# First projections of a two-block network: loaded, ordered and multiplied tile by tile of x

## The chip, the core and the metric

The kernel runs on one core of a Trainium2 chip. The core has five engines that work beside each other, each through its own queue in order: PE (matrix products; PEld is its weight load), DVE (vector work), ACT (activation functions, copies with a scale), POOL (a second, slower vector engine) and SP, which issues most loads here. Sixteen DMA engines move the data. The metric is device time in microseconds from the first to the last instruction of one execution and what lies around it, as the median of several runs.

## What is computed

Two blocks in a row on x of 512 tokens and 1024 channels, all in fp32. The first block has two layers of the following kind; the second block (a recurrence beside sparse attention) does not touch the change.

```python
n = rmsnorm(h, attn_norm[l])
proj = n @ w_in[l]
u, v_sgu, q, k, v_att = split(proj)          # 512 columns each
y_sgu = sgu_mixer(gelu(u), gelu(v_sgu), ...)
y_att = diff_attention(rope(q), rope(k), v_att, ...)   # 4 heads, two maps of 64 each
h = h + concat(y_sgu, y_att) @ w_out[l]
h = h + conv_ffn(rmsnorm(h, ffn_norm[l]), ...)
```

In `rmsnorm` each token's row is divided by its root mean square. The kernel multiplies first and applies that factor, which is one number per token, to the products afterwards.

## The kernel before, in words

x is held transposed as `h`, eight tiles of 128 channels by 512 tokens. Products are made in a fast fp32 format: every operand is split into a high part and a low part, and `mm3` makes three products (high by high, high by low, low by high) that add up in one PSUM bank. So each weight passes through `prep` (line 257 and after): SP loads 128 x 1024 into `raw`, POOL writes the high part `whi` (`gscale`, line 204), DVE subtracts to get the low part `wlo` (`tt`, line 192). There are three buffers of each of the three. A tile of x is split in `split_scaled`: ACT writes the high part with the norm's gain (line 298), DVE the low part (line 197). `Next` (line 771) does that for a tile and adds the tile's squares to a running sum (ACT squares, POOL adds, DVE adds the last).

The kernel is written for a planner: instructions get a priority by their place in the program, `tc.high_priority(offset=...)` moves a stretch ahead by that many places (nested offsets add up; `prep` has 260), and the planner puts, on each engine, the ready instruction with the best priority next. On the chip each engine then keeps that order. Tiles with the same tag take turns in so many buffers.

`program` first loads the columns `vec` and the first tile of x at a high priority, and the rest of `vec`. `enter(stack, "one", ...)` gives the first block eight PSUM banks: three `mm`, two `sc`, two `tr`, one `o`. Then, at line 779, a loop loads the other seven tiles of x and calls `Next` on all eight. `mixer` for layer 0 begins with the tables of the rotation (`tables`, DVE and ACT); `fm` multiplies queries and keys of head 0 over all eight tiles of x into the two `sc` banks (line 569); `norm_row` sums the squares over channels with four small products (`columns`, line 333), takes root and reciprocal (`rstd_col`, lines 336 and 337: the column `rc`) and spreads it to rows with four transposes (`spread`, line 358); ACT copies the result to `R` (line 573). The rotation tables CR and SR are multiplied by R (DVE, POOL). `q_of` and `k_of` rotate: `rope` copies the product, shuffles it, multiplies by CR and SR and adds, in buffers with the tag `rp`, of which there are four; the result is split again, and `stacked` (lines 431, 432) moves the halves with small loads into tiles with the tag `QK`, of which there are twelve. After that the values: 96 products, four token tiles by eight tiles of x, into three `mm` banks and the `o` bank; ACT copies them out scaled by `rc` (line 589) and DVE makes the low part.

Then the steps of `STEPS` are written: `k1` makes queries and keys of head 1 in `mm` banks, `a0` is the attention of head 0 (its scores at lines 450 and 451, in `sc` banks), `a1` that of head 1, `v0` the first half of the gate (`gate_half`, two `mm` banks), and so on. `silu_c` (lines 613 to 615) is a small vector that the second block's modulation needs later.

Of the kernel before, what the change touches and what calls it, by code (L numbers as in the profile page):

```python
# [5 lines left out]
F32 = mybir.dt.float32  # L6
# [3 lines left out]
ALU = mybir.AluOpType  # L10
# [134 lines left out]
def program(tc, a, at, out):  # L145
# [3 lines left out]
    def nm(s):  # L149
        count[0] += 1  # L150
        return f"{s}_{count[0]}"

    import contextlib
    with contextlib.ExitStack() as ctx:
# [13 lines left out]
        def bank(tag="mm"):  # L168
            return scope["ps"].tile([P, 512], F32, tag=tag, name=nm(tag), bufs=scope["banks"][tag])

        def t2(tag, dt=F32R):
            return tl([P, 512], dt, tag)
# [23 lines left out]
        def stt(o, i0, s, i1, op0, op1, **kw):  # L196
            latest[0] = V.scalar_tensor_tensor(o, i0, s, i1, op0, op1, **kw)  # L197
# [5 lines left out]
        def gscale(o, i, s, plus=0.0):  # L203
            G.tensor_scalar(o, i, s, plus, op0=ALU.mult, op1=ALU.add)  # L204

        def fr(ap):
            return ap.bitcast(F32)
# [2 lines left out]
        h = ctile([P, KD, S], "h")  # L210
        vec = ctile([P, a["vec"].shape[1]], "vec")
        with tc.high_priority(offset=5000):
            nc.sync.dma_start(vec[:, 0:KD], a["vec"][:, 0:KD])
            nc.sync.dma_start(h[:, 0, :], a["x"][:, 0, :])

        nc.sync.dma_start(vec[:, KD:], a["vec"][:, KD:])

        def col(n, j=0, w=1):
            return vec[:, at[n] + j:at[n] + j + w]
# [7 lines left out]
        with tc.high_priority(offset=5000):  # L227
            G.memset(eps, EPS)
            A.activation(eps[:, 1:2], eps[:, 0:1], AF.Sin)
        eps = eps[:, 0:1]  # L230

        AHEAD = 260
        HALVES = slice(0, 256), slice(256, 512)
# [42 lines left out]
        def mm3(o, sh, sl, mh, ml, first, last):  # L276
            T.matmul(o, sh, mh, start=first, stop=False)  # L277
            T.matmul(o, sh, ml, start=False, stop=False)  # L278
            T.matmul(o, sl, mh, start=False, stop=last)  # L279
# [13 lines left out]
        def fm(src, X, tag="mm"):  # L293
            return fm_group([src], X, [tag])[0]
# [176 lines left out]
        def recurrence_constants():  # L471
# [23 lines left out]
            V.tensor_scalar(hb[:, 0:4], col("lru_ba", 0, 4), 0.5, None, op0=ALU.mult)  # L495
            V.tensor_scalar(hb[:, 4:8], col("lru_bx", 0, 4), 0.5, None, op0=ALU.mult)


        def mixer(l, X, sums, on_h):
            li = LAM_INIT[l]  # L500
# [65 lines left out]
                    tt(V, OT[hd], OT[hd], spread(SL[:, 4 * hd:4 * hd + 4], "o"), ALU.mult)  # L566


            oq = fm(a[f"w_q{l}"][0], X, "sc")
            ok = fm(a[f"w_k{l}"][0], X, "sc")  # L570
            rc, Rp = norm_row(sums, "tr")
            R = row()
            A.copy(R, Rp)
            tt(V, CR, CR, R, ALU.mult)
            tt(G, SR, SR, R, ALU.mult)
            qks = q_of(oq), k_of(ok)
            os = [bank(t) for t in ("mm", "mm", "mm", "o")]
            for c in range(4):
                w = prep(a[f"w_va{l}"][c])
                for kk in range(2):  # L580
                    k = 2 * c + kk
                    for t in range(NT):
                        tok = slice(t * P, t * P + P)
                        n = slice(kk * 512, kk * 512 + 512)
                        mm3(os[t], X[k][0][:, tok], X[k][1][:, tok], w[0][:, n], w[1][:, n], k == 0, k == KD - 1)
            VA = []
            for t in range(NT):
                hi, lo = t2("V"), t2("V")
# [18 lines left out]
            A.activation(lv[:, 2:4], lv[:, 0:2], AF.Exp)  # L607
            tt(V, lv[:, 4:5], lv[:, 3:4], lv[:, 2:3], ALU.subtract)
            V.tensor_scalar(lv[:, 5:6], lv[:, 4:5], -li, None, op0=ALU.add)
            V.tensor_scalar(lv[:, 6:7], col(f"subln{l}"), 1.0 - li, None, op0=ALU.mult)  # L610
            nlam, sub = lv[:, 5:6], lv[:, 6:7]
            if l == 0:
                A.activation(silu_c, col("c", 0, KD), AF.Tanh, scale=0.5)
                stt(silu_c, silu_c, 1.0, col("c", 0, KD), ALU.add, ALU.mult)
                V.tensor_scalar(silu_c, silu_c, 0.5, None, op0=ALU.mult)

            VT = []

# [152 lines left out]
        class Next:  # L771
# [3 lines left out]
            def __call__(self, m):  # L775
                self.X[m] = split_scaled(h[:, m, :], col(self.gain, m), "X")
                self.sums.square(h[:, m, :])

        nx = Next("attn_norm0")
        for m in range(KD):  # L780
            if m > 0:
                nc.sync.dma_start(h[:, m, :], a["x"][:, m, :])
            nx(m)
        fin = [None, None]

        def last(m, ts=slice(0, 512)):
# [586 lines left out]
```

## Time and profile before

| | |
|---|---|
| median of 3 runs | 1817.63 us (1812.58 to 1818.64) |
| the profiled execution | 1814.92 us |
| its span, first to last instruction | 1813.3 us |
| PE busy | 1737.3 us (96%) |
| DVE, POOL, ACT busy | 1253.4, 808.4, 588.2 us |

Busy times of the engines overlap. PE is near its whole span, so what matters is where it is not busy, or busy at half its clock. A line of the timeline reads: start, duration (of the whole run of instructions where there are several), engine, line, operation, output tile <- input tiles, shapes, count, and in brackets how long the engine was idle before and what ended that.

### The profile page before, as it was taken

How to read it: one execution, taken by the hardware profiler on the slowest of the kernel's cores; microseconds unless marked ns; L12 is line 12 of the kernel's file. 1: busy time of each engine (PE TensorE's matmuls, PEld its weight loads, DVE VectorE, ACT ScalarE, POOL GpSimd, SP SyncE). 2: the span in 40 equal slices, each digit the busy share in tenths (PEclk: the TensorE clock that was granted, in tenths of full speed). 3: DMA queues.
4: the chain of work that ended last, by engine and by line, in shares of the span. 5: the costliest groups of instructions: out<-in, count | busy, mean ns of one | idle time of the engine just before them, and what ended most of it. 6: DMA issues, size and time to landing. Idle time of an engine off the chain costs nothing. (4 is left out here: it accounts for less than half of the span.)

```text
span 1813.3 us, 23607 instructions
## 1 busy us (share of the span) xinstructions
PE 1737.3 (96%) x8422; PEld 1448.9 (80%) x8422; DVE 1253.4 (69%) x1957; ACT 588.2 (32%) x1120; POOL 808.4 (45%) x791
## 2 busy tenths in 40 slices
PE   7999999999999999999999999899898899999997
PEld 5887778888887888787888887878776788888886
DVE  7677788868877578769868967655876872444344
ACT  3464332113123256332203213344774431201022
POOL 5553554346446454444426626322461752323233
PEclk9999999999999999999999999899999899999998
DMA  4552255657745453245567756375331223323331
GB/s 174 155 140 94 93 185 175 215 189 232 252 152 173 133 150 93 96 132 177 176 216 233 235 175 192 105 251 192 129 116 49 104 82 104 93 94 98 99 94 58
DMA packets 104117, 267.74 MB, mean 148 GB/s; under 512 B 12481, under 2 KB 15553, under 8 KB 104001
## 3 DMA queue, kind: packets, MB, share of 16 engines
q1 hardware_dynamic: 104000, 266.25, 46.5%
q8 instruction: 66, 1.08, 0.2%
q14 instruction: 51, 0.41, 0.1%
HBM read 213.77 MB, written 35.65 MB: 138 GB/s over the span
## 5 line engine op out<-in xcount | busy, mean ns | idle before, releaser
L204 POOL TENSOR_SCALAR whi<-raw 128x1024 fp32r<-128x1024 f32 (+3 forms) x266 | 313.9, 1185 | 630.8 <-PE mm L278 227.3
L192 DVE TENSOR_TENSOR wlo<-raw,whi 128x1024 fp32r<-128x1024 f32 (+3 forms) x264 | 383.9, 1456 | 186.7 <-POOL whi L204 171.5
L277 PE MATMUL mm<-X,whi 128*128 128x512 f32 (+1 forms) x688 | 261.9, 386 | 6.6 <-ACT X L298 2.0
L279 PE MATMUL mm<-X,wlo 128*128 128x512 f32 (+1 forms) x688 | 261.7, 383 | 5.1 <-DMA wlo<-parts 2.8
L278 PE MATMUL mm<-X,whi 128*128 128x512 f32 (+1 forms) x688 | 263.9, 385 | 1.0 <-DVE X L197 1.0
L197 DVE SCALAR_TENSOR_TENSOR p<-p,vec,p 128x512 f32<-128x512 f32 x176 | 183.8, 1066 | 4.2 <-ACT p L711 3.3
L277 PEld LDWEIGHTS mm<-X,whi 128*128 128x128 f32 x688 | 130.2, 192 | 32.7 <-ACT X L298 2.6
L279 PEld LDWEIGHTS mm<-X,wlo 128*128 128x128 f32 x688 | 131.7, 192 | 30.3 <-DVE wlo L192 4.4
L278 PEld LDWEIGHTS mm<-X,whi 128*128 128x128 f32 x688 | 131.7, 191 | 25.3 <-DVE X L197 2.6
L277 PE MATMUL sc<-X,whi 128*128 128x512 f32 (+1 forms) x376 | 143.3, 383 | 7.3 <-POOL whi L204 7.2
L711 ACT ACTIVATE p<-p,vec 128x512 f32<-128x512 f32 x88 | 69.9, 813 | 241.6 <-DVE p L192 236.4
L279 PE MATMUL sc<-X,wlo 128*128 128x512 f32 (+1 forms) x376 | 141.6, 380 | 5.4 <-DVE wlo L192 4.4
L278 PE MATMUL sc<-X,whi 128*128 128x512 f32 (+1 forms) x376 | 142.2, 379 | 0.0
L192 POOL TENSOR_TENSOR pt<-pt,pt 128x512 fp32r<-128x512 f32 x64 | 109.9, 1719 | 62.6 <-ACT pt L250 62.3
L277 PE MATMUL tr<-X,whi 128*128 128x512 f32 x280 | 108.9, 389 | 0.0
L278 PE MATMUL tr<-X,whi 128*128 128x512 f32 x280 | 108.9, 389 | 0.0
L279 PE MATMUL tr<-X,wlo 128*128 128x512 f32 x280 | 107.6, 390 | 0.0
L277 PEld LDWEIGHTS sc<-X,whi 128*128 128x128 f32 x376 | 72.2, 192 | 20.5 <-POOL whi L204 7.8
L279 PEld LDWEIGHTS sc<-X,wlo 128*128 128x128 f32 x376 | 71.5, 191 | 21.2 <-DVE wlo L192 8.5
L455 ACT ACTIVATE p<-p,sa 128x128 f32<-128x128 f32 (+3 forms) x128 | 71.6, 561 | 51.0 <-DVE sa L453 50.5
L192 POOL TENSOR_TENSOR p<-p,p 128x512 f32<-128x512 f32 x44 | 60.7, 1379 | 58.7 <-ACT p L718 37.2
L278 PEld LDWEIGHTS sc<-X,whi 128*128 128x128 f32 x376 | 71.9, 191 | 12.7
(691 smaller groups left out, 4014.6 us busy)
## 6 DMA issues: line engine op xcount, KB each, us to landing
parts<-pt SPq DMA_DIRECT2D x128, 256.0 KB, 3.9
raw<-in_w_f_dram SPq DMA_DIRECT2D x64, 512.0 KB, 3.7
vt<-in_ada_dram SPq DMA_DIRECT2D x96, 256.0 KB, 3.0
raw<-in_w_g_dram SPq DMA_DIRECT2D x44, 512.0 KB, 3.5
raw<-in_w_v_dram SPq DMA_DIRECT2D x44, 512.0 KB, 4.2
raw<-in_w_d_dram SPq DMA_DIRECT2D x32, 512.0 KB, 4.2
whi<-parts SPq DMA_DIRECT2D x32, 512.0 KB, 3.4
wlo<-parts SPq DMA_DIRECT2D x32, 512.0 KB, 4.2
```

The lines of the kernel that those rows point to most:

```text
L192: i = e.tensor_tensor(o, i0, i1, op=op)
L197: latest[0] = V.scalar_tensor_tensor(o, i0, s, i1, op0, op1, **kw)
L204: G.tensor_scalar(o, i, s, plus, op0=ALU.mult, op1=ALU.add)
L277: T.matmul(o, sh, mh, start=first, stop=False)
L278: T.matmul(o, sh, ml, start=False, stop=False)
L279: T.matmul(o, sl, mh, start=False, stop=last)
L455: A.activation(p[i], p[i], AF.Exp, bias=m, scale=-1.0, accum_out=Z[:, z0 + i:z0 + i + 1])
L711: A.activation(y, t[:, 0:512], AF.Identity, bias=col(f"cb{l}", j), scale=col(f"cw{l}0", j))
```

## The change

The loop over the tiles of x now does, for each tile: its load, its split and squares, the three products each of head 0's queries and keys, and the twelve of the values. Queries and keys of head 0 are loaded in two halves of 512 columns (`head_qk`, for tiles 0 to 3 and 4 to 7), which are split into tiles with the tag `QK` and not into `whi` and `wlo`; each value weight serves two tiles of x. The loop stands under a priority raised by 3000. Six PSUM banks are taken for it ahead of the loop. Eleven small products of `ones` with itself go into a `tr` bank ahead of it. The first columns of `vec` are loaded from ACT's queue, and the rest of `vec` behind the first halves of the weights. Three small DVE products are pinned behind the DVE instruction written last before them (`here`). Layer 1 does the same work as before in the same order.

```diff
@@ program
         with tc.high_priority(offset=5000):
-            nc.sync.dma_start(vec[:, 0:KD], a["vec"][:, 0:KD])
+            nc.scalar.dma_start(vec[:, 0:KD], a["vec"][:, 0:KD])
             nc.sync.dma_start(h[:, 0, :], a["x"][:, 0, :])
-
-        nc.sync.dma_start(vec[:, KD:], a["vec"][:, KD:])
...
+        HEAD = [{}, {}]
+
+        def head_raw(src, n=512):
+            raw = wp.tile([P, 1024], F32, tag="raw", name=nm("raw"), bufs=3)[:, :n]
+            nc.sync.dma_start(raw, src)
+            return raw
+
+        def head_qk(z):
+
+            c = slice(512 * z, 512 * z + 512)
+            for n in "qk":
+                raw = head_raw(a[f"w_{n}0"][0][:, c])
+                hi, lo = t2("QK"), t2("QK")
+                gscale(hi, raw, 1.0)
+                tt(V, lo, raw, fr(hi), ALU.subtract)
+                HEAD[z][n] = hi, lo
...
+        def values_of(os, X, w, k):
+            n = slice(k % 2 * 512, k % 2 * 512 + 512)
+            for t in range(NT):
+                tok = slice(t * P, t * P + P)
+                mm3(os[t], X[k][0][:, tok], X[k][1][:, tok], w[0][:, n], w[1][:, n], k == 0, k == KD - 1)
@@ mixer
-            oq = fm(a[f"w_q{l}"][0], X, "sc")
-            ok = fm(a[f"w_k{l}"][0], X, "sc")
+            if l == 0:
+                oq, ok = first_os[:2]
+            else:
+                oq = fm(a[f"w_q{l}"][0], X, "sc")
+                ok = fm(a[f"w_k{l}"][0], X, "sc")
             rc, Rp = norm_row(sums, "tr")
...
-            os = [bank(t) for t in ("mm", "mm", "mm", "o")]
-            for c in range(4):
-                w = prep(a[f"w_va{l}"][c])
-                for kk in range(2):
-                    k = 2 * c + kk
-                    for t in range(NT):
-                        tok = slice(t * P, t * P + P)
-                        n = slice(kk * 512, kk * 512 + 512)
-                        mm3(os[t], X[k][0][:, tok], X[k][1][:, tok], w[0][:, n], w[1][:, n], k == 0, k == KD - 1)
+            os = first_os[2:] if l == 0 else [bank(t) for t in ("mm", "mm", "mm", "o")]
+            for k in range(KD if l else 0):
+                if k % 2 == 0:
+                    w = prep(a[f"w_va{l}"][k // 2])
+                values_of(os, X, w, k)
...
-            V.tensor_scalar(lv[:, 6:7], col(f"subln{l}"), 1.0 - li, None, op0=ALU.mult)
+            with here():
+                V.tensor_scalar(lv[:, 6:7], col(f"subln{l}"), 1.0 - li, None, op0=ALU.mult)
             nlam, sub = lv[:, 5:6], lv[:, 6:7]
             if l == 0:
                 A.activation(silu_c, col("c", 0, KD), AF.Tanh, scale=0.5)
-                stt(silu_c, silu_c, 1.0, col("c", 0, KD), ALU.add, ALU.mult)
-                V.tensor_scalar(silu_c, silu_c, 0.5, None, op0=ALU.mult)
+                with here():
+                    stt(silu_c, silu_c, 1.0, col("c", 0, KD), ALU.add, ALU.mult)
+                    V.tensor_scalar(silu_c, silu_c, 0.5, None, op0=ALU.mult)
@@ program, ahead of the layers
+        warm = bank("tr")
+        with tc.high_priority(offset=4000):
+            for _ in range(11):
+                T.matmul(warm[:, 0:P], ones, ones, start=True, stop=True)
         nx = Next("attn_norm0")
-        for m in range(KD):
-            if m > 0:
-                nc.sync.dma_start(h[:, m, :], a["x"][:, m, :])
-            nx(m)
+        first_os = [bank(t) for t in ("sc", "sc", "mm", "mm", "mm", "o")]
+        with tc.high_priority(offset=3000):
+            w_va = None
+            for m in range(KD):
+                if m > 0:
+                    nc.sync.dma_start(h[:, m, :], a["x"][:, m, :])
+                if m % 4 == 0:
+                    head_qk(m // 4)
+                if m == 0:
+                    nc.sync.dma_start(vec[:, KD:], a["vec"][:, KD:])
+                nx(m)
+                for o, n in zip(first_os, "qk"):
+                    w, c = HEAD[m // 4][n], slice(m % 4 * P, m % 4 * P + P)
+                    mm3(o, w[0][:, c], w[1][:, c], *nx.X[m], m == 0, m == KD - 1)
+                if m % 2 == 0:
+                    w_va = prep(a["w_va0"][m // 2])
+                values_of(first_os[2:], nx.X, w_va, m)
```

## Rows read from the trace of the kernel before

**Rows 1.** The page's first part: busy time, share, instructions of each engine.

```profile
PE 1737.3 (96%) x8422; PEld 1448.9 (80%) x8422; DVE 1253.4 (69%) x1957; ACT 588.2 (32%) x1120; POOL 808.4 (45%) x791
```

**Rows 2.** Windows: stretch, length, busy PE PEld DVE ACT POOL, clock, DMA share, GB/s.

```profile
0.00:60.00 60.00, 48.05 (x190) 37.25 (x191) 40.24 (x48) 23.99 (x36) 32.88 (x34) 0.97 0.54 174
60.00:182.00 122.00, 118.82 (x701) 103.17 (x700) 90.69 (x212) 62.48 (x136) 56.88 (x51) 1.00 0.44 123
182.00:700.00 518.00, 511.81 (x2388) 424.75 (x2387) 405.66 (x569) 157.91 (x277) 258.92 (x231) 1.00 0.56 175
```

**Rows 3.** Windows again, one microsecond after the stall; the granted clock is third from last.

```profile
36.00:37.00 1.00, 1.00 (x4) 0.74 (x3) 0.77 (x1) 0.00 (x0) 0.00 (x0) 0.50 0.88 348
```

**Rows 4.** Timeline of the first 8 us, all engines.

```profile
0.81 0.40 SPq L213 DMA_DIRECT2D vec<-in_vec_dram  x1
...
3.78 5.79 SPq L782 DMA_DIRECT2D h<-in_x_dram  x7
4.72 0.72 ACT L298 ACTIVATE X<-h,vec 128x512 fp32r<-128x512 f32 x1 [2.42 <-DMA h<-in_x_dram]
...
6.00 1.13 POOL L204 TENSOR_SCALAR whi<-raw 128x1024 fp32r<-128x1024 f32 x1 [3.47 <-DMA raw<-in_w_q_dram]
...
7.18 0.80 PE L277 MATMUL sc<-X,whi 128*128 128x512 f32 x1 [7.18 <-POOL whi L204]
```

**Rows 5.** Timeline at the end of the values and the start of head 1.

```profile
52.38 0.47 PE L277 MATMUL mm<-X,whi 128*128 128x512 f32 x1
...
54.06 0.68 ACT L589 ACTIVATE V<-mm,rc 128x512 fp32r<-128x512 f32 x1
...
54.97 0.74 DVE L197 SCALAR_TENSOR_TENSOR V<-mm,rc,V 128x512 fp32r<-128x512 f32 x1
```

**Rows 6.** Timeline of the column sums, `rc` and R.

```profile
28.46 1.05 PE L333 MATMUL tr<-ones,acc 128*128 128x1 f32 x8
...
31.99 1.28 ACT L336 ACT_TABLE_LOAD   x1
...
33.28 0.26 ACT L336 ACTIVATE rc<-tr,eps 128x4 f32<-128x4 f32 x1
...
35.48 0.17 DVE L337 RECIPROCAL rc<-rc 128x4 f32<-128x4 f32 x1
...
40.77 0.60 PE L358 MATMUL tr<-ident,rc 128*128 128x128 f32 x4
...
41.40 0.58 ACT L573 COPY R<-tr 128x512 f32<-128x512 f32 x1 [7.85 <-PE tr L358]
```

**Rows 7.** Timeline of PE: products in a row, early and later, and a single one.

```profile
12.05 1.48 PE L277 MATMUL mm<-whi,X 128*128 128x512 f32 x3
...
29.70 0.39 PE L279 MATMUL o<-whi,X 128*128 128x512 f32 x1
...
29.93 0.84 PE L277 MATMUL mm<-whi,X 128*128 128x512 f32 x3
...
36.91 0.63 PE L277 MATMUL mm<-whi,X 128*128 128x512 f32 x1
```

**Rows 8.** Timeline of the stall before 34.5 us.

```profile
26.62 2.70 POOL L204 TENSOR_SCALAR whi<-raw 128x1024 fp32r<-128x1024 f32 x2 [3.40 <-PE sc L278]
...
33.22 2.34 DVE L192 TENSOR_TENSOR wlo<-raw,whi 128x1024 fp32r<-128x1024 f32 x2
...
34.49 0.50 PE L278 MATMUL mm<-wlo,X 128*128 128x512 f32 x1 [3.49 <-DVE wlo L192]
```

**Rows 9.** Timeline of PE, plain fp32 products of 128 columns, two passes each.

```profile
159.17 2.62 PE L661 MATMUL mm<-ws,vt 128*128 128x128 f32 x22
```

**Rows 10.** Timeline: the last small load for head 0's keys, its first scores.

```profile
58.52 0.59 SPq L432 DMA_DIRECT2D QK<-rp  x1
...
63.35 0.39 PE L450 MATMUL sc<-QK,QK 128*128 128x512 f32 x1
```

**Rows 11.** DMA issues up to 60 us: count, KB each, median us to landing.

```profile
QK<-rp SPq DMA_DIRECT2D x12, 128.0 KB, 2.4
```

## The prediction

> **What bounds the kernel now.** I read the page first: PE is busy 96% of the span [rows 1], so time can come out only where PE idles or runs slowly. The wide windows say where that is: from 182 to 700 us PE idles 6 of 518 us, from 60 to 182 it idles 3.2 of 122, but in the first 60 it idles 12 [rows 2]. In the midst of those, from 36 to 37, the granted clock is 0.50, the lower level of 1.2 GHz [rows 3]. Then the timeline. The first product starts at 7.18, released by POOL's split of the first query weights [rows 4]; the first product of head 1's queries starts at 52.38 [rows 5]. Between lie 48 products for queries and keys of head 0, 96 for the values, and two small groups, column sums (1.05) and transposes (0.60) [rows 6]. At full clock two products start 0.227 us apart (three in 0.84, the last of which lasts 0.39), at half clock 0.43 (three in 1.48, the last 0.63) [rows 7]. So 144 x 0.227 + 1.65 = 34.3 us are needed, and 52.4 - 34.3 = 18.1 are lost: 7.2 before the first product; 3.5 waiting for the low part of a value weight [rows 8]; some 3.3 by products at half clock, nine intervals before 15.4 and seven after that stall, at 0.20 more each; the rest, about 4, in waits for weights between 7.2 and 11.5 and in two waits of half a microsecond.
>
> The 3.5 us stall has a cause that the change removes. There are three `whi` buffers; queries and keys hold two until all eight tiles of x are multiplied, so the second value weight gets its buffer late: POOL waits 3.40 us for a query product, then splits, and DVE's subtraction follows [rows 8].
>
> **Part by part.**
> *Start.* The gain columns go out on ACT's queue, so x and the weights go out one issue (0.40) earlier; the query weight comes as a half. ACT's first X starts at 4.72 and POOL gets the 512 KB query weight at 6.00 [rows 4], so 512 KB take 1.28, a half 0.64. It is there at 6.00 - 0.64 - 0.40 = 5.0, POOL splits half the width in 0.57 (half of 1.13 [rows 4]), and PE starts at 5.5. Key half and first value weight follow: 5.0 + 0.64 + 1.28 = 6.9, split 1.13, low part 1.2 (DVE's pairs of these take 2.34 [rows 8]): 9.2. By then ten products are done (2.3 us), so 1.4 us are waited.
>
> *Warm-up.* Eleven fp32 products of 128 columns are 22 passes, 0.119 each at full clock (22 in 2.62 [rows 9]); double that, an estimate for half clock, is 5.2, from about 1 us (the queues start at 0.81 [rows 4], and `ones` has to be set) to 6.3 at most. They lie where PE has nothing else, though at that bound the first product moves from 5.5 to 6.3. Before, the first products ran at half clock; I take the first tile to run at full clock now. Bounds: 0 to 1.8 saved (nine intervals), by whether the wait in tile 0 undoes it.
>
> *Tiles.* The other 134 products take 30.4 us if fed: the last value product at 39.6. Per tile PE needs 18 x 0.227 = 4.1 us; SP issued seven tiles of x in 5.79, 0.83 each [rows 4]; and per pair of tiles POOL has one whole split (1.13), DVE one subtraction (1.2 [rows 8]) and two low parts of X, against 8.2 us of PE. The halves live in the QK buffers, so the values have three `whi` buffers and no 3.5 us stall remains, nor the half clock behind it.
>
> *Tail of the tiles: the new wait.* The loop stands under a priority raised by 3000; the column sums of `norm_row` do not. Before, those sums ran at 28.46, ahead of most value products [rows 6]. Now every product of the loop goes ahead of them whenever it is ready, and from tile 1 on one always is; so they run after 39.6. The value banks can't be emptied before `rc` is there (their copy scales by it), and head 1's products need those banks. In a row: sums 1.05, square root 0.26, reciprocal 0.17 [rows 6], value copy 0.68, low part 0.74 [rows 5], handovers of 0.03 to 0.16: 3.2 us. Head 1 starts at 42.8 instead of 52.4, 9.6 earlier; PE idles 1.6 in this, beside sums and transposes. The root's table load (1.28 [rows 6]) I cost at nothing, since ACT is idle ahead of it and PE still multiplies; uncovered it costs 1.3.
>
> *What is late next.* R, the row of inverse norms, comes 0.60 (transposes) and 0.58 (copy) after `rc`: 39.6 + 1.05 + 0.26 + 0.17 + 1.2 + handovers = 42.5, or 43.2 behind one value copy. Before, it was there at 41.98 [rows 6]. **R gains nothing.** From R to the scores of head 0 runs one chain: SR times R on POOL, two POOL steps, copy and subtraction for the query, the same again for the key (its copy waits for the query's `rp` buffers), then eight small loads on SP. The last is issued at 58.52 [rows 10] and, with 2.4 us to land [rows 11], is there near 61.5: 19.5 after R. The scores started at 63.35, so there were about 2 us of slack. Now they are ready at 62.0 to 62.7, while head 1's products (63.35 - 52.38 = 11.0) are over at 53.8. PE is left with 8 to 9 us, to be filled from `gate_half`: 48 of its products of 256 columns (half of 0.227, so 5.5 us) fit the one free `mm` bank; the second becomes free only when head 1's queries have passed the same `rp` buffers. So some 3 us idle. Against before, PE at 62.4 has done all that it had done at 63.35, and 5.5 us more: gain 6.5. An idle of this size may bring the half clock again, as the 3.5 us stall did [rows 3]: 1.4 off, bounds 0 to 1.8. That makes 5.1 to 6.5. The mixer's rest has 3.2 us of PE idle and DVE at 74% from 60 to 182 [rows 2]; with less spare PE work there, 0 to 2 go back. **Sum: 5 us**, from 3 to 7.
>
> *At nothing:* the `here()` pins only keep small vec products from standing ahead of weight splits on DVE, and the rest of vec, now behind the first weights on SP, is first wanted by a small Tanh; `values_of` for layer 1 is the same work.
>
> **The sum and the runs.** The profiled execution took 1814.92 (a span of 1813.3 and 1.6 around it); the median of the runs is 1817.63, 2.7 above it. The four times average 1815.9; less 5 gives **1811**.
>
> **Rivals.**
> 1. *The sums find a gap.* Were they put into PE's queue amid the tiles, `rc` and R would be there when the last product ends: only a wait of 0.5 as before is left, head 1 starts near 40.3, 12 earlier, and the chain to the scores starts near 37 with the query's product and is ready at 57, covered by head 1 and `gate_half`. Less a give-back of 1: 1815.9 - 11 = 1805. For it: PE does wait in tile 0. Against: the sums need all eight squares, and were not ready before 28 in the trace [rows 6], when PE has a backlog.
> 2. *The scores stand ahead of the filler.* PE works in queue order. If the scores follow head 1's products directly, PE stands from 53.8 to 62.4 and of the 9.6 us gained only 1 is left; the half clock takes that: 1816. For it: they did so before [rows 10].
> 3. *Slower: R is late.* When R is wanted, ACT has four value copies (0.68 each [rows 5]) and DVE two weight subtractions for head 1 (2.34 [rows 8]) ready. If R's copy and products queue behind them with the table load uncovered, R comes 2.7 + 2.3 + 1.3 = 6.3 later, the scores near 69, and with rival 2's order PE loses some 6 and the half clock's 1.4: 1823. It decides from R about 5.5 us later than the 42.0 of before; below that it stays within rival 2.
> 4. *Slower: the tiles starve.* If every product of the tiles waits on a load and PE falls to 0.43 per product, the last ends at 9.2 + 134 x 0.43 = 66.8, head 1 starts near 70, 17 later than before: 1833. The Trainium skill ("TensorE: Matmul & The Clock Gate", section "Loop structure matters more than you think") warns of this loop: a transfer waited for between bursts of matmuls sends PE back to the half clock. Against it: a tile of x is issued every 0.83 [rows 4], and PE takes 4.1 for it.
> 5. *It doesn't do what it says:* the first value weight comes so late that the tiles are not multiplied side by side, and only the start's 1.6 are gained: 1814.
>
> **How the numbers follow.** Forecast 0.45, rivals 0.20, 0.20, 0.08, 0.02 and 0.05. A measurement of this kernel tells about 0.3% (5.5 us) from no change. The forecast lies 6.6 under the median, so a little over half of its chance counts as faster (0.27), with rival 1 0.47; the rest of it with most of rivals 2 and 5 is 0.42 within 0.3%; rivals 3 and 4 and a little of rival 2 are 0.11. The range runs from rival 1 less 2 us to rival 2 plus 2 (the step from the profile to the median), and leaves out rivals 3 and 4 and the edges: 1803 to 1818.
>
> **What would show it.** First product near 5.5 to 6.3; no PE wait for `whi` or `wlo` between 10 and 39; last value product near 40 and the column sums behind it; PE idle about 1.6 there; scores at 62 to 63 with `gate_half` products ahead of them. Wrong would be: sums amid the tiles (rival 1), one long PE wait at the scores (rival 2), R after 47 (rival 3), products 0.43 apart after 12 us (rival 4).

## The result: 0.7% slower

The changed kernel takes 1827.29 us (median of 5 runs, 1825.58 to 1830.35) against 1816.47 for the kernel before on the same chip (5 runs). The ratio is 1.0066 (95% interval 1.0048 to 1.0084): some 11 us slower, where 1811 and at most 1818 were forecast. The profiled execution has a span of 1828.6 us.

The page shows the same picture as [rows 1]: PE still 96% busy. Three windows of the changed kernel (stretch, length, busy PE PEld DVE ACT POOL, clock, DMA share, GB/s), to be laid beside [rows 2]:

```profile
0.00:60.00 60.00, 53.33 (x229) 43.45 (x230) 42.41 (x46) 22.32 (x34) 34.31 (x37) 0.97 0.53 173
60.00:182.00 122.00, 112.63 (x644) 97.32 (x642) 86.19 (x203) 66.30 (x137) 55.87 (x51) 0.96 0.44 124
182.00:700.00 518.00, 511.58 (x2378) 424.39 (x2377) 403.67 (x555) 150.34 (x261) 257.53 (x230) 1.00 0.55 174
```

Up to 60 us PE is busy 5.3 us longer than before, but 5.04 of its 53.33 are the warm-up, and products at half clock count for longer. The lead in work is read off the places instead: head 1's first product starts 3.6 us earlier (48.75 against 52.38). Between 60 and 182 PE then idles 9.4 us (before 3.2) and its clock falls from 1.00 to 0.96. From 182 to 700 nothing has changed. So the start delivered a part of its lead, and the mixer of layer 0 lost more than that.

The start itself, in the timeline of the changed kernel (PE, and ACT for R; compare [rows 4, 5, 6 and 8]):

```profile
1.09 5.04 PE L805 MATMUL tr<-ones 128*128 128x128 f32 x22 [1.09 <-POOL ones L221]
6.50 0.50 PE L292 MATMUL sc<-X,QK 128*128 128x512 f32 x1 [0.37 <-POOL QK L204]
...
28.40 0.50 PE L294 MATMUL sc<-X,QK 128*128 128x512 f32 x1 [2.88 <-DVE QK L192]
...
45.36 0.95 PE L348 MATMUL tr<-ones,acc 128*128 128x1 f32 x8
46.96 0.62 PE L373 MATMUL tr<-ident,rc 128*128 128x128 f32 x4 [0.66 <-DVE rc L352]
47.62 0.59 ACT L597 COPY R<-tr 128x512 f32<-128x512 f32 x1
48.75 0.47 PE L292 MATMUL mm<-X,whi 128*128 128x512 f32 x1 [1.17 <-DVE V L197]
```

The first product starts at 6.50 instead of 7.18, head 1 at 48.75 instead of 52.38. The last value product starts at 45.1 instead of 51.9 and the column sums stand behind the tiles, as forecast; the last of head 0's query and key products, which are spread over all tiles, starts at 42.4 instead of 27.5, and R's copy at 47.62 instead of 41.40. (Where values or head 0's products are said to end, below too, it is the start of the last of them.) The 2.88 us wait is new. It comes from the second key half, in the timeline of POOL and DVE:

```profile
21.93 1.06 POOL L204 TENSOR_SCALAR QK<-raw 128x512 fp32r<-128x512 f32 x1
...
24.22 1.51 DVE L423 TENSOR_SCALAR rp<-rp,vec 128x512 f32<-128x512 f32 x1
25.77 1.15 DVE L424 TENSOR_SCALAR rp<-rp 128x512 f32<-128x512 f32 x1
26.84 1.51 DVE L192 TENSOR_TENSOR QK<-raw,QK 128x512 fp32r<-128x512 f32 x1
```

POOL has split it at 23.0; DVE's subtraction, which PE needs, runs only at 26.84, behind two steps of the rotation's tables (lines 423 and 424). A window behind the wait:

```profile
30.00:35.00 5.00, 5.00 (x17) 3.94 (x16) 5.00 (x7) 0.30 (x1) 1.38 (x1) 0.67 0.53 191
```

Its clock is 0.67, so part of it ran at the lower level of 1.2 GHz.

Where do the 10 us of the mixer go? Two landmarks serve for all kernels below. One is DVE's reciprocal in `attend`, which ends a head's softmax. The other is the first transpose of `silu_c` behind the mixer; the warm-up left out, it stands at the same place of PE's queue in both programs, so PE has done the same work there. Kernel before, then the changed kernel:

```profile
81.48 0.20 DVE L542 RECIPROCAL sa<-sa 128x8 f32<-128x8 f32 x1 [3.90 <-ACT p L455]
102.98 0.19 DVE L542 RECIPROCAL sa<-sa 128x8 f32<-128x8 f32 x1
121.76 0.20 DVE L542 RECIPROCAL sa<-sa 128x8 f32<-128x8 f32 x1 [1.11 <-ACT p L455]
144.05 0.20 DVE L542 RECIPROCAL sa<-sa 128x8 f32<-128x8 f32 x1
181.32 0.60 PE L358 MATMUL o<-ident,silu_c 128*128 128x128 f32 x4
```

```profile
80.39 0.20 DVE L563 RECIPROCAL sa<-sa 128x8 f32<-128x8 f32 x1
111.08 0.18 DVE L563 RECIPROCAL sa<-sa 128x8 f32<-128x8 f32 x1
133.70 0.19 DVE L563 RECIPROCAL sa<-sa 128x8 f32<-128x8 f32 x1
155.26 0.20 DVE L563 RECIPROCAL sa<-sa 128x8 f32<-128x8 f32 x1 [1.68 <-ACT p L470]
191.45 0.60 PE L373 MATMUL o<-ident,silu_c 128*128 128x128 f32 x4
```

Head 0 ends 1 us earlier than before, head 1 8 us later, head 2 12 later, the mixer 10.1 later. In layer 1 the first of these transposes starts at 754.6 (before 744.5): the 10 us are handed through. The two profiled executions differ by 15.3 us in span; the other 5 arise behind that. The profiled execution is the slowest of its five runs, and what is to be explained is the 11 us of the medians.

### The profile page after: what moved, and what is told of

It reads as the page before. It is cut to its first block, busy times and chain, and to the rows that moved or that the text cites. A ratio compares the mean times of both kernels' runs of the same rounds, so it can differ in the third digit from the quotient of the medians.

```text
span 1828.6 us, 23674 instructions
## 1 busy us (share of the span) xinstructions
PE 1747.4 (96%) x8444; PEld 1458.4 (80%) x8444; DVE 1256.7 (69%) x1959; ACT 593.5 (32%) x1123; POOL 810.7 (44%) x793
## 3 DMA queue, kind: packets, MB, share of 16 engines
q1 hardware_dynamic: 104144, 266.25, 45.8%
## 5 line engine op out<-in xcount | busy, mean ns | idle before, releaser
L294 PE MATMUL sc<-X,wlo 128*128 128x512 f32 (+1 forms) x360 | 134.7, 378 | 4.4 <-DVE wlo L192 4.4
L292 PE MATMUL sc<-X,whi 128*128 128x512 f32 (+1 forms) x360 | 136.2, 379 | 0.0
L293 PE MATMUL sc<-X,whi 128*128 128x512 f32 (+1 forms) x360 | 135.5, 376 | 0.0
L204 POOL TENSOR_SCALAR p<-p,sa 128x512 f32<-128x512 f32 (+1 forms) x96 | 63.1, 675 | 50.9 <-DVE sa L192 16.3
L197 DVE SCALAR_TENSOR_TENSOR vt<-vt,rp 128x512 f32<-128x512 f32 x96 | 80.5, 872 | 0.0
```

## The experiments

Each ratio is to the kernel before on the same chip, with its 95% interval; "R" and "mixer end" are the starts of R's copy and of the transposes of `silu_c` in the profiled execution. That is one of the runs, and the runs of one kernel spread by 3 to 12 us (the trace of e4_values_low is its slowest, 1821.33), so the mixer's end and the median of a row need not belong together to the microsecond.

| run | median us | ratio | R | mixer end |
|---|---|---|---|---|
| changed kernel | 1827.29 | 1.0066 (1.0048 to 1.0084) | 47.6 | 191.4 |
| e1_sums_first | 1826.49 | 1.0059 (1.0044 to 1.0075) | 39.7 | 190.3 |
| e2_no_warmup | 1824.19 | 1.0044 (1.0027 to 1.0061) | 47.2 | 191.3 |
| e3_before_sums_last | 1845.82 | 1.0169 (1.0151 to 1.0187) | 54.2 | 199.6 |
| e4_values_low | 1811.90 | 0.9985 (0.9971 to 0.9999) | 39.0 | 177.4 |
| e5_halves_early | 1824.91 | 1.0063 (1.0043 to 1.0084) | 45.8 | 191.9 |
| e11_qk_then_r | 1810.71 | 0.9985 (0.9970 to 1.0000) | 40.0 | 179.3 |
| e6_before_less_filler | 1823.67 | 1.0049 (1.0031 to 1.0068) | 42.9 | 192.9 |
| e9_after_less_filler | 1817.93 | 1.0014 (1.0001 to 1.0027) | 47.5 | 181.4 |
| e7_after_1023 | 1809.92 | 0.9984 (0.9968 to 0.9999) | 46.6 | 176.1 |
| e7_before_1023 | 1812.10 | 0.9994 (0.9980 to 1.0009) | 42.0 | 178.0 |
| e8_after_2310 | 1820.60 | 1.0034 (1.0018 to 1.0050) | 47.2 | 181.5 |
| e8_before_2310 | 1820.52 | 1.0036 (1.0014 to 1.0057) | 42.6 | 185.8 |
| e9_tail_pinned | 1830.76 | 1.0090 (1.0077 to 1.0103) | 47.6 | 191.0 |
| e12_gelu_behind_head2 | 1819.16 | 1.0029 (1.0014 to 1.0044) | 46.9 | 184.5 |
| e12_gate_early | 1820.48 | 1.0031 (1.0016 to 1.0046) | 41.4 | 187.9 |
| e10_no_warmup_1023 | 1810.49 | 0.9976 (0.9965 to 0.9986) | 46.7 | 176.7 |
| e10_halves_early_1023 | 1812.53 | 0.9990 (0.9979 to 1.0002) | 45.9 | 175.1 |
| e11b_qk_r_1023 | 1814.70 | 1.0003 (0.9992 to 1.0013) | 39.6 | 182.3 |

### First theory: R is late

R comes 6.2 us later and heads 1 to 3 end 8 to 12 later: theory A says that R's lateness is handed down the attention chain; theory B, that the planner has put the mixer into a worse order, whatever R does.

```diff
 # e1, in the changed kernel
-            rc, Rp = norm_row(sums, "tr")
-            R = row()
-            A.copy(R, Rp)
+            with (tc.high_priority(offset=5000) if l == 0 else contextlib.nullcontext()):
+                rc, Rp = norm_row(sums, "tr")
+                R = row()
+                A.copy(R, Rp)
 # e2, in the changed kernel
-            for _ in range(11):
-                T.matmul(warm[:, 0:P], ones, ones, start=True, stop=True)
 # e3, in the kernel before: norm_row and the rotation of head 0 written behind the values, and
+            with (tc.issue_after(lastmm[0].ins) if l == 0 else contextlib.nullcontext()):
+                rc, Rp = norm_row(sums, "tr")
 # e4, in the changed kernel: out of the raised loop, and for layer 0 where layer 1 has them
-                if m % 2 == 0:
-                    w_va = prep(a["w_va0"][m // 2])
-                values_of(first_os[2:], nx.X, w_va, m)
-            for k in range(KD if l else 0):
+            for k in range(KD):
```

> The changed kernel, with one thing altered: the column sums, root and transposes of layer 0 and the copy to R stand under a priority raised by 5000, so that they go amid the tiles. Theory A (R is late: the chain from R to the scores of the heads sets the end of the first mixer): R moves from 48.2 to about 37 us, the transposes of silu_c, with which the first mixer ends, from 191.4 to 181 or earlier, and the time falls from 1827 to 1808 to 1814. Theory B (the raised priorities made the planner find a worse order inside the mixer, whatever R does): R moves just as much, but the mixer ends near 190 and the time stays between 1822 and 1830.

R was 8 us earlier and nothing followed: theory A fails in this form. Head 0's products now ended at 45.2, so the rotation could start no sooner.

> The changed kernel without the eleven products of ones, whose result nothing reads. Both theories: the first products run at half clock as they did before the change; 18 products at 0.20 more each end the tiles up to 3.6 us later, and under theory A all of it is added to R and to the time: 1829 to 1831. If the 2.9 us wait of PE at 25 us hides it, 1827.

Both theories missed: without the warm-up the kernel is not slower.

> The kernel before, with one thing altered: the column sums of layer 0 are pinned behind the last value product on PE, and the rotation of head 0 is written behind the values. Weights, loads, clock and priorities are those of before. Theory A: R moves from 42.0 to about 56, the scores of head 0 from 63.4 to 73 or later, the mixer ends 8 to 12 us later and the time is 1824 to 1829. Theory B: the order inside the mixer is made anew but nothing pushes it to be worse; 1814 to 1820.

Delaying R by 12.8 us in the kernel before cost 30 us, more than either theory had; the mixer ends 18.3 later, so the rest arose behind it.

> The changed kernel, with the value products (and the loads and splits of their weights) taken out of the raised priority and written behind the rotation, as before the change; queries and keys stay in the tile loop with their halves, warm-up and loads stay. Theory A: the sums are free to go when ready, R comes at 38 to 41, and with the value weights no longer short of buffers the time is 1808 to 1814. Theory B: 1822 to 1830.

With the values behind, head 0's products end at 22.7 and R comes at 39.0: the loss is gone. I mended theory A to A': the chain starts at the later of R and the end of head 0's products. e5 (second halves loaded at tile 2 instead of 4) moves the products alone, e11 moves both, by another way.

```diff
 # e5, in the changed kernel
-                if m % 4 == 0:
-                    head_qk(m // 4)
+                if m in (0, 2):
+                    head_qk(m // 2)
 # e11: e4 without the warm-up, tables and norm_row of layer 0 under an offset of 5000, and
+                with (tc.issue_after(r_end) if l == 0 and k >= 3 else contextlib.nullcontext()):
+                    values_of(os, X, w, k)
```

> The changed kernel with the second halves of head 0's query and key weights loaded at the third tile of x instead of the fifth; nothing else differs. Theory A' (the layer-0 mixer ends when its chain ends: R and head 0's products, rotation, stacked loads, softmax head by head): the 2.9 us wait on the second key half and the half clock behind it go, head 0's products end near 38 to 39 us instead of 42.4, R's copy starts near 44 instead of 47.6, the mixer ends 3 to 5 us earlier than in the changed kernel: 1822 to 1825 us. Rival B' (the planner's order inside the mixer costs the 10 us whatever the chain's start): within 1.5 us of the changed kernel, 1825 to 1829.

The products ended at 25.7 and R came 1.9 earlier; the mixer's end and the ratio stayed. The 2.88 us wait went, but a wait of 1.85 for the low part of a value weight came in its place. A' can live with this run only because R is still late.

> The changed kernel without the warm-up products, with the values written behind the rotation again (as in the kernel with the values low), the rotation's tables and the row R at the highest priority, and the value products from the fourth tile on held behind R's transposes on TensorE: both starts of the chain early at once (head 0's products end near 23 us, R's copy starts near 34 to 35 us against 39.0 with the values low and 41.4 before). Theory A': the mixer ends up to 4 us earlier than with the values low, as far as TensorE's 3 us of idle time there allow: 1807 to 1811. Theory B' or a bound by TensorE: the same as with the values low, 1811 to 1813.

Both are earlier than in the changed kernel, and the time is low again, though R came at 40.0 and not at 34 to 35 and the products ended at 30.7 and not near 23. So far the slower kernels have a late R or late products and the faster ones neither, as A' has it. But B fits as well: each edit changed what the planner had to order.

### The test that broke it: less work for PE

In layer 0's `gate_half` the third product of each group (low part of X by high part of the weight) is left out, 64 products of 256 columns, 7.3 us of PE, none on the chain:

```diff
-                            mm3(os[t // 2][:, m], X[k][0][:, tok], X[k][1][:, tok], w[0][:, n], w[1][:, n],
-                                k + t % 2 == 0, k + t % 2 == KD)
...
+                            T.matmul(os[t // 2][:, m], X[k][0][:, tok], w[0][:, n], start=f, stop=False)
+                            T.matmul(os[t // 2][:, m], X[k][0][:, tok], w[1][:, n], start=False, stop=e)
```

> The kernel before; in layer 0's gate_half the third product (weights' high part by the low part's partner in X) of each group of three is left out: 64 products of 128x256, at half of the 0.227 us of a 128x512 product some 7.3 us of TensorE, none of it on the attention chain. If the mixer were bound by TensorE's work, as the prediction took it, layer 0 ends 6 to 7.3 us earlier: 1808 to 1810 us. Theory A' (the chain sets the end, TensorE's slack is small only because the filler was cut to fit): 0 to 3 us earlier, 1812 to 1816.

> The changed kernel with the same 64 products of layer 0's gate_half left out. Bound by TensorE's work: 6 to 7.3 us earlier than the changed kernel, 1819 to 1821. Theory A': the chain is 6 us later there and TensorE already idles 9.4 us between 60 and 182 us, so 0 to 2 us earlier: 1824 to 1828, and TensorE's idle time in the mixer grows by 5 us or more.

Nobody had this: with less work the kernel before becomes 9 us *slower*, though its R moved by 1.5 us only, and the changed kernel 9 us faster, though its R stays late. Head 3's softmax ends at 160.4 in the one and at 156.1 in the other, and their mixers end at 192.9 and 181.4. So the start alone doesn't decide, and A' falls as the whole account. What else differs is the order in which the program has the mixer's work. In PE's queue the last head's product with the values stands at place 749 in the kernel before and the gating products end at 743; in the changed kernel it is 786 and 728, with products of `w_o` between. In e6 it is 721 of a queue shorter by 64, which answers to 785. But e9_after_less_filler has it at the same place as e6 and is faster, so this place by itself isn't the cause.

### One written order for both starts

If the order makes the loss, a change without any work in it that gives the changed kernel another order must take the loss away. Softmax goes through the four row tiles of a head in the order 3, 2, 1, 0; other orders are as good:

```diff
-            for i in (3, 2, 1, 0):
+            for i in sm_order[0]:
...
+            sm_order[0] = (1, 0, 2, 3) if l == 0 else (3, 2, 1, 0)
```

> The changed kernel; in layer 0 alone the softmax of a head goes through its four row tiles in the order 1, 0, 2, 3 instead of 3, 2, 1, 0. The work is the same, and the start up to R is untouched. The written program's order on TensorE becomes that of the kernel before at the mixer's end: the last head's products with the values end at place 750 of the queue (kernel before 749, changed kernel 786), the gating products end at 744 (743 and 728). Theory B'' (the 10 us come from this order, which the planner chose when the start was made over): near the kernel before, 1815 to 1819 us, mixer end near 182. Theory A' (R and head 0's products, 6 us later, set it): as the changed kernel, 1824 to 1828, mixer end 188 to 191.

> Control: the kernel before with the same order of row tiles in layer 0's softmax. Its order on TensorE at the mixer's end stays what it was (750 and 743). Both theories: within 2 us of the kernel before, 1813 to 1817 us.

> The changed kernel with the row tiles of layer 0's softmax in the order 2, 3, 1, 0: a second way to the same end (the last head's value products end at place 756, the gating products at 744). Theory B'': 1815 to 1820 us. Theory A': 1824 to 1828.

> Control for it: the kernel before with the row tiles in the order 2, 3, 1, 0 (752 and 743). Both theories: 1813 to 1817 us.

In both pairs the changed start is as fast as the old one: 1809.9 and 1812.1, 1820.6 and 1820.5. Softmax ends and mixer ends of the first pair in the timeline, changed start first, each with its window from 60 to 182:

```profile
81.01 0.20 DVE L566 RECIPROCAL sa<-sa 128x8 f32<-128x8 f32 x1 [0.28 <-ACT p L472]
108.00 0.19 DVE L566 RECIPROCAL sa<-sa 128x8 f32<-128x8 f32 x1
120.32 0.20 DVE L566 RECIPROCAL sa<-sa 128x8 f32<-128x8 f32 x1 [0.88 <-ACT p L472]
142.50 0.20 DVE L566 RECIPROCAL sa<-sa 128x8 f32<-128x8 f32 x1
176.05 0.60 PE L373 MATMUL o<-ident,silu_c 128*128 128x128 f32 x4
```

```profile
60.00:182.00 122.00, 119.41 (x704) 103.26 (x703) 93.59 (x220) 67.20 (x145) 59.25 (x55) 1.00 0.45 126
```

The same of the control:

```profile
77.79 0.20 DVE L545 RECIPROCAL sa<-sa 128x8 f32<-128x8 f32 x1 [0.88 <-ACT p L457]
98.34 0.20 DVE L545 RECIPROCAL sa<-sa 128x8 f32<-128x8 f32 x1
123.52 0.20 DVE L545 RECIPROCAL sa<-sa 128x8 f32<-128x8 f32 x1 [0.52 <-ACT p L457]
145.58 0.20 DVE L545 RECIPROCAL sa<-sa 128x8 f32<-128x8 f32 x1
177.99 0.60 PE L358 MATMUL o<-ident,silu_c 128*128 128x128 f32 x4
```

```profile
60.00:182.00 122.00, 120.88 (x718) 106.10 (x717) 94.14 (x217) 66.04 (x140) 59.66 (x54) 1.00 0.44 124
```

With R at 46.6, a microsecond earlier than in the changed kernel, head 2 ends at 120.3 instead of 133.7 and the mixer 15 us earlier; PE idles 2.6 us instead of 9.4, at full clock. The second pair shows the other side: an order costs the old start 6 us too. So a start as late as this doesn't cost the 11 us in every order; they come with the order that the planner chose when the start was made over. What is held here is the written order of the softmax. The planner's queues still differ within a pair (head 1's softmax ends at 108.0 and 98.3 in the first, at 111.0 and 104.4 in the second), and no run gives the changed kernel the very queues of the kernel before. All four times lie outside what was expected: e7_before_1023 and e8_after_2310 by less than 1 us, e7_after_1023 by 5 on the fast side, and the control e8_before_2310, with the last head at place 752 and the gating products at 743, by 3.5 on the slow side. The places at the queue's end, by which I had chosen these orders, don't tell a good one from a bad one.

### What in the order costs the time

```diff
 # e9_tail_pinned, in the changed kernel, around the first group of w_o
+                with (tc.issue_after(last_av[0]) if l == 0 and m0 == 0 else contextlib.nullcontext()):
...
 # e12_gelu_behind_head2, in the changed kernel, around the Gelu evacuations of gate_half
+                    with (tc.issue_after(exps[2]) if l == 0 and z == 1 else contextlib.nullcontext()):
...
 # e12_gate_early, in the kernel before
-            for step in STEPS.split():
+            for step in (STEPS.replace(" v1", "").replace(" a2", " v1 a2") if l == 0 else STEPS).split():
```

> The changed kernel with the first w_o products of layer 0 held on TensorE behind the last head's last product with the values; nothing else differs (that product stands at place 750 of the queue instead of 786, the gating products still end at 728). If the end of the order alone costs the 10 us: mixer end 182 to 185, 1816 to 1820 us. If the loss is made in the middle (head 1's softmax ends 8 us later and head 2's 12 us later than before) and the w_o products only fill the wait: TensorE then waits where they stood, mixer end 191 or later, 1826 to 1831 us.

Not the end: the `w_o` products there only filled a wait. The loss is made in the middle, where heads 1 and 2 fall back. ACT's timeline of the changed kernel there: the end of head 2's exponentials (`p<-p,sa`) with the gate's second Gelu evacuation (`vt<-mm,rc`, the copy of its products out of PSUM through Gelu) among them. At each change between the exponential and Gelu an ACT_TABLE_LOAD runs, the load of the other function's table.

```profile
121.48 0.73 ACT L470 ACTIVATE p<-p,sa 128x512 f32<-128x512 f32 x1 [1.05 <-DVE sa L468]
...
122.32 1.28 ACT L656 ACT_TABLE_LOAD   x1
123.61 0.84 ACT L656 ACTIVATE vt<-mm,rc 128x256 f32<-128x256 f32 x2
124.47 1.28 ACT L470 ACT_TABLE_LOAD   x1
125.77 0.62 ACT L470 ACTIVATE p<-p,sa 128x384 f32<-128x384 f32 x1
...
127.02 1.28 ACT L656 ACT_TABLE_LOAD   x1
128.31 0.84 ACT L656 ACTIVATE vt<-mm,rc 128x256 f32<-128x256 f32 x2
...
130.65 1.28 ACT L470 ACT_TABLE_LOAD   x1
131.94 0.51 ACT L470 ACTIVATE p<-p,sa 128x256 f32<-128x256 f32 x1
...
132.97 0.39 ACT L470 ACTIVATE p<-p,sa 128x128 f32<-128x128 f32 x1
```

Four exponentials that take 2.3 us are spread over 11.9, with four table loads between. The Trainium skill ("ScalarE: Activation LUTs", section "Table sets: the hidden batching unit") says to put activations of one table set together, and here one sees why; its section "What ACT_TABLE_LOAD costs" adds a drain of 1.38 us to each load, which the trace doesn't show (the load at 124.47 takes 1.28, the exponential starts at 125.77).

> The changed kernel; in layer 0 the Gelu evacuation of the gate's second half is held on ScalarE behind head 2's last exponential (in the changed kernel it stands between them, with four table loads of 1.28 us around it). The plan of TensorE's end is remade with it (last head's value products at place 771; changed kernel 786, kernel before 749). If the collision makes the loss: head 2's softmax ends at 121 to 127 us instead of 133.7, mixer end 181 to 186, 1815 to 1821 us. If not: 1825 to 1830.

The same four exponentials and the Gelu behind them, in this kernel:

```profile
122.88 0.72 ACT L472 ACTIVATE p<-p,sa 128x512 f32<-128x512 f32 x1 [1.04 <-DVE sa L470]
...
123.83 0.62 ACT L472 ACTIVATE p<-p,sa 128x384 f32<-128x384 f32 x1
...
126.01 0.51 ACT L472 ACTIVATE p<-p,sa 128x256 f32<-128x256 f32 x1 [0.57 <-DVE sa L470]
...
126.74 0.40 ACT L472 ACTIVATE p<-p,sa 128x128 f32<-128x128 f32 x1
...
128.55 1.57 ACT L660 ACTIVATE vt<-mm,rc 128x256 f32<-128x256 f32 x4
```

Head 2's softmax ends at 127.3 instead of 133.7, the mixer 6.9 us earlier, the kernel takes 8 us less. Head 1 ends as late as in the changed kernel (112.5 against 111.1).

> The kernel before, its start untouched; layer 0's step for the gate's second half is written ahead of heads 2 and 3 instead of behind them. The same work; ScalarE's Gelu evacuation and the Gelu of the u products then stand between head 2's exponentials, and the last head's value products at place 785. If such an order costs the time, whatever the start: as slow as the changed kernel or slower, mixer end 188 to 196, 1822 to 1832 us. If the order is harmless without a late start: 1812 to 1817.

With its start untouched (R at 41.4, head 1's softmax at 103.0 as before) the kernel before gets Gelus among head 2's exponentials, ends head 2 at 146.3 instead of 121.8, and loses 5.4 us; I had expected at least 7. So such an order costs time by itself.

Head 1's 8 us (111.1 against 103.0) are another matter. The last small load of its rotated keys and the first scores of head 2, in the kernel before and then in the changed kernel:

```profile
77.51 0.60 SPq L432 DMA_DIRECT2D QK<-rp  x1
105.58 0.39 PE L450 MATMUL sc<-QK,QK 128*128 128x512 f32 x1
```

```profile
84.86 0.58 SPq L447 DMA_DIRECT2D QK<-rp  x1
108.48 0.63 PE L465 MATMUL sc<-QK,QK 128*128 128x512 f32 x1
```

Head 1's keys come 7.3 us later, behind those of head 0, whose last load goes out at 63.9 instead of 58.5; in e7_after_1023 and e12_gelu_behind_head2 they come as late (85.1 and 85.6), and head 1 ends late there too. This much of theory A holds. But it is not handed on whole: head 2's scores start only 2.9 us later than before, and then head 2 takes 25.2 us to the end of its softmax where it took 16.2. Of its 12 us, 9 arise in its own softmax.

All twenty traces divide by this. Where no table load stands among head 2's eight exponentials (the kernel before, e4, both e7, e8_before, both e10, e11, e11b and e12_gelu_behind_head2), 9.8 to 12.6 us pass from the start of the first to that of the last; where four or six do (the other ten), it is 18.7 to 22.3. All ten of these are slower than the kernel before (by the ratios' intervals), with an early start (e6, e12_gate_early: 1.0049 and 1.0031) as with a late one; of the first ten two are (e8_before_2310 1.0036, e12_gelu_behind_head2 1.0029), and the late starts among them go from 0.9976 to 1.0029. So this collision goes with most of the loss, but it isn't all that an order can cost. How the 11 us divide to the microsecond stays open, as holding the Gelu also made the planner's order behind it anew.

### What the start is worth with that order

> The changed kernel with row tiles in the order 1, 0, 2, 3 in layer 0 and without the 11 warm-up products. Against 1809.9 with them: if the warm-up's earlier full clock is kept to the end, 1.5 to 3 us later; if it is lost in later waits, the same within 1.5 us. I take the second: 1809 to 1812 us.

> The changed kernel with row tiles in the order 1, 0, 2, 3 in layer 0 and the second halves of head 0's query and key weights loaded at the third tile of x. The tiles then end 1.9 us earlier (43.3 against 45.1 in the pair without the order). If the lead of TensorE at the start is kept when the order is held: 1807 to 1809 us against 1809.9; if not, 1809 to 1812.

Both are e7_after_1023 with one more edit (the warm-up out; e5's halves). Mixer ends of 176.7 and 175.1 against 176.1 and times within 3 us of each other: by the mixer's end the warm-up brings 0.6 us there, the earlier halves 0.9, though that kernel's median is 2.6 us longer. Neither is told from nothing in the runs.

> The kernel with head 0's products first, R early and the values behind it (1810.7 us), with row tiles in the order 1, 0, 2, 3 in layer 0. The order brought the kernel before 2 us and the changed one 17; the plan of this one already ends like that of the kernel before (749), so 0 to 3 us: 1807 to 1811 us.

A miss. The order 1, 0, 2, 3, which brought the changed kernel 15 to 17 us (by the ratios and by the medians), costs e11 3 to 4. An order is good or bad for one kernel, not in itself. The lowest ratios are those of the changed kernel with that order, with the warm-up (0.9984) or without (0.9976), 3 to 4 us under the kernel before; e4 and e11 (0.9985) can't be told from them.

## Why the prediction was wrong, point by point

*Start and tiles.* First product forecast at 5.5 to 6.3, measured 6.50. The tiles were forecast to end at 39.6; the column sums right behind them start at 45.36. The step "if fed" failed: the tiles were not always fed. Of the 5.8 us, 2.9 are the wait on the second key half, whose subtraction I hadn't followed past the rotation's tables on DVE, 1.0 is the later start, and some 1.6 the lower clock behind the wait (5 us at 0.67). Elsewhere products follow each other as [rows 7] have them at full clock (value products start at 11.08, 11.31 and 11.54), so rival 4 is out.

The Trainium skill's warning ("TensorE: Matmul & The Clock Gate", section "Loop structure matters more than you think") was of waits for transfers in such a loop; none of PE's waits in the tiles is put down to a transfer, and the longest was for DVE.

*Column sums* behind the tiles: right. From there to head 1's start 3.2 us were forecast and 3.4 measured (45.36 to 48.75).

*R gains nothing*: it came 6.2 later than before, as the tiles ended later than forecast. This was the condition of rival 3 ("R about 5.5 us later"), and its 1823 is the nearest number I gave. But rival 3 has PE wait for head 0's scores, and no long wait of PE stood there: they started at 63.45, as before, with `gate_half` products ahead of them. So rival 3's mechanism didn't do it, and its near number is luck; rival 2 is out as well. What came late behind R was head 1 (its keys by 7.3 us), which I had not followed: I took the chain as far as head 0's scores and no further. That by itself doesn't cost the time: e7_after_1023, with R at 46.6 and head 1's keys as late, has the lowest median of the table.

*"PE at 62.4 has done all that it had done at 63.35, and 5.5 us more"*: the gain of 6.5 is measured as 3.6. Head 1 started 6.0 us later than the forecast 42.8, by the tiles; the 3 us of idle time ahead of the scores, which I had taken off, did not occur and made good half of that.

*"With less spare PE work there, 0 to 2 go back"*: **this is the step that failed.** 3.6 + 10.1 = 13.7 us went back. From 60 us to the mixer's end, in the kernel before and then in the changed kernel:

```profile
60.00:181.32 121.32, 118.14 (x695) 102.54 (x694) 90.16 (x211) 62.44 (x135) 56.88 (x51) 1.00 0.44 124
```

```profile
60.00:191.45 131.45, 122.08 (x680) 104.89 (x678) 91.15 (x215) 68.47 (x140) 55.87 (x51) 0.95 0.41 115
```

PE idled 9.4 us where it had idled 3.2, which makes 6.2; and 131 us at a mean clock of 0.95 lose, as an estimate, some 6.6 more, where before the clock stood at 1.00. So the waits and the clock took about half each. I had treated the mixer as a store of PE work in which a lead keeps its worth, and its order as given. But the order is the planner's, made for the whole program at once; and PE, ACT and DVE keep it on the chip, so a softmax that falls behind holds the heads behind it while each engine's queue goes on in the order planned. A rival "the mixer is ordered anew" with a price on either side was missing. Its size can be read off the runs: orders with the same work and the same start gave 1812.1 and 1820.5 in the kernel before, and 1809.9, 1820.6 and 1827.3 in the changed one.

*What the start is worth.* In the two pairs the changed start ends the mixer 1.9 and 4.3 us earlier and the kernel 2.2 earlier and 0.1 later, with some 3 us of uncertainty on each. A gain of 5 would fit one pair at its edge and not the other.

## What to carry to other kernels

Where a planner orders the program, an edit at one place remakes the order of everything behind it: compare the queues of the two programs first, and price a new order as a rival of its own, here 3 to 17 us either way. A stage that is 96% busy isn't a store of work into which a lead can be paid: a head's softmax that falls behind costs PE idle time and then clock. Before a time is put down to an edit, try the edit in more than one order, by a change without work in it, applied to both kernels. And look for table loads among the exponentials of a softmax that others wait for.

## What I had not expected of the hardware

- PE's clock in the mixer fell behind waits of PE, but the sum of the idle time doesn't tell it. With 9.4 us idle between 60 and 182 it is 0.96, with 2.6 us 1.00; yet e8_after_2310 idles 6.4 us at 1.00, and e3_before_sums_last 5.9 at 0.96. In the changed kernel it is at the lower level from 108.5 to 111.5, behind a PE wait of 2.11 us that ended at 106.62, from 166.5 to 169.5, behind one of 0.96 that ended at 165.82, and for most of the window from 180 to 190, around waits of 1.16 (ended at 178.39) and 0.78 us (ended at 181.27):

```profile
180.00:190.00 10.00, 9.22 (x37) 7.26 (x35) 5.76 (x18) 2.16 (x3) 0.00 (x0) 0.66 0.00 1
```

- A warm-up of 22 passes in 5.04 us gave nearly full clock from the first tile (three value products take 0.96 us at 9.13, and 1.49 at 9.93 in e2 without it), and nothing at the end (e2, e10_no_warmup_1023).
